# Block 2's convolution as products on TensorE, with another order of the mixers' other work and all weight splits on VectorE

## The chip, the cores and the metric

The kernel runs on one core of a Trainium2 chip. The metric is the device time of one execution in microseconds (us). Engines are named as in the profile: PE is TensorE (matrix products), PEld its loading of weights, DVE is VectorE, ACT is ScalarE, POOL is GpSimd, SP is the engine whose queue issues the loads. PEclk is the granted clock of TensorE as a share of its full 2.4 GHz; 0.5 is its lower level, 1.2 GHz.

## The reference

The program is two transformer-like blocks over 256 tokens of width 1024, each followed by a mixture of experts (MoE). The change touches mainly Block 2. There one input projection of the normalised tokens feeds three mixers: a memory cross-attention, a conformer convolution over 384 channels, and a bidirectional RWKV-7 scan. Their outputs are joined, projected, added to the stream, and go into the second MoE. The convolution, cut:

```
def conformer_conv(pc, conv_w, conv_b, ln_g, ln_b):
    val, gate = jnp.split(pc, 2, axis=-1)
    u = val * jax.nn.sigmoid(gate)
    u = lax.conv_general_dilated(u, conv_w[:, None, :], window_strides=(1,),
        padding=[(CONV_PAD, CONV_PAD)], ..., feature_group_count=CONV_WIDTH) + conv_b
    ...
    return jax.nn.silu(uf)
```

It is depthwise: each of the 384 channels has its own 31 taps over the tokens, 15 to either side, and channels don't mix.

## The kernel before

**Stages.** Block 1's projections and mixers run to about 470 us of the trace, its MoE from 450 to 925, Block 2's mixers from 925 to 1265, the second MoE from 1265 to the end. Both MoE stages stream expert weights from HBM in pieces of 1 MB.

**Projections.** `dense_T` and `dense_N` compute in fp32 accuracy by splitting both operands into a high and a low part: three products for each tile (high by high, low by high, high by low). The weights' halves come from `split_w`: ScalarE copies the loaded weights `wc` into `whi` (L161), and a subtraction (L162) gives `wlo`. A counter, `nsplit`, sends every third subtraction to GpSimd and the others to VectorE.

**Block 2's mixers.** `b2_mixers` writes the instructions. Three pairs of projections (`self.pairs`) come first. Then six RWKV chains (`rw_stages`) of some 43 steps each start at steps 0, 4, 9, 15, 19 and 24. A chain begins with its decay gates (products `ps_lw` at L1794 and L1795, tanh at L1798), builds matrices from them, solves small triangular systems by repeated products (`ps_lv`, `rAW`, `rX`), and ends in outputs of 64 columns (`ps_Y`, `ps_S`, `ps_YS`). The products of a chain are small, 64x64 in four positions of the array, and VectorE or ScalarE must move each result before the next product can start. From step 1 on, at every second step, one closure of the list `fill` is written between: further pairs of projections, `b2_attention`, `b2_conv_in` and the three `b2_conv_gate` (the convolution's input, 128 channels each, into `U`), later the loads for the output projection, two early pieces of the second MoE, and the router's preparation. From step 17 on each chain step also takes one tap of the convolution.

**The convolution.** `b2_conv_taps(j0, j1)` does one tap for the three groups of 128 channels. Groups 0 and 1 are one multiply and add each on VectorE (L1649). Group 2 is a scaled copy on ScalarE (L1652) and an addition on GpSimd (L1653). The taps' factors are a per-partition scalar in `cwT`, made in `b2_vectors`. `b2_conv_norm` then normalises the channels.

**What sets the order.** The written order is the start; a scheduler over a simulated timeline moves instructions of each engine within what their inputs and buffers allow. SP's queue runs in order: a load that waits for its buffer holds all loads behind it. The second MoE takes its pieces in the ring order `ORDER2`: two from the small pool `early` (slots `a` and `b`), then slots `r` and numbered slots that come free as the mixers end. The last product of the output projection of Block 2 is `psl` at L2150 and L2151.

Of the kernel before, what the change touches and what calls it, by code (L numbers as in the profile page):

```python
# [18 lines left out]
class K:  # L19
    def __init__(self, ctx, tc, ins, out, dbg=None):  # L20
        self.ctx, self.tc, self.nc, self.I, self.out = ctx, tc, tc.nc, ins, out
        self.dbg = dbg or {}
        self.pools = {}
        self.nsplit = 0
        self.order, self.mixing, self.inorder = None, False, False
        self.cst = self.open("cst", 1)
        self.x = self.cst.tile([P, 2, D], FT, name="x")
# [119 lines left out]
    def split_w(self, wt, kc, n):  # L147
# [3 lines left out]
        for k0 in range(0, kc, step):  # L151
# [1253 lines left out]
    def b2_vectors(self):  # L1405
# [27 lines left out]
        self.cwT = c.tile([P, 3, 31], FT, name="cwT")  # L1433
        nc.vector.tensor_copy(self.cwT, pc)
# [28 lines left out]
    def block2(self):  # L1463
# [15 lines left out]
        self.pairs = [(p, self.b2_proj_load(p)) for p in ((9, 10), (0, 3), (6, 7))]  # L1479
# [17 lines left out]
    TAP0, TAP1, TAPN = 17, 17, 1  # L1497

    def b2_mixers(self):

        self.keys = {}
        for pair, wt in self.pairs:
            self.b2_rwkv_proj(pair, wt)
        chains = [(self.OFF[i], self.rw_stages(i % 2, i // 2)) for i in range(6)]
        fill = [lambda: self.b2_rwkv_proj((1, 4)), lambda: self.b2_rwkv_proj((2, 5)),
                lambda: self.b2_rwkv_proj((8, 11)), self.b2_attention, self.b2_conv_in]
        fill += [lambda c=c: self.b2_conv_gate(c) for c in range(3)]
        taps = [lambda j=j: self.b2_conv_taps(j, min(j + 1, 31)) for j in range(31)] + [self.b2_conv_norm]
# [131 lines left out]
    def b2_conv_taps(self, j0, j1):  # L1640
        nc, tp = self.nc, self.tp
        Y = self.cvY
        for j in range(j0, j1):
            for c in range(3):
                u, w = self.U[:, c, j:j + 256], self.cwT[:, c, j:j + 1]
                if j == 0:
                    nc.vector.tensor_scalar(Y[:, c], u, w, self.v2["cvb"][:, c:c + 1], op0=OP.mult, op1=OP.add)
                elif c < 2:
                    nc.vector.scalar_tensor_tensor(Y[:, c], u, w, Y[:, c], op0=OP.mult, op1=OP.add)  # L1649
                else:  # L1650
                    t = tp.tile([P, T], FT, name="cvt", tag="cvt")
                    nc.scalar.activation(t, u, AF.Copy, scale=w)  # L1652
                    nc.gpsimd.tensor_tensor(Y[:, c], Y[:, c], t, op=OP.add)  # L1653
# [727 lines left out]
```

## Time and profile before

| | us |
|---|---|
| median of 3 runs | 1729.07 |
| lowest and highest | 1726.86, 1734.26 |
| the profiled execution | 1733.84 |
| its span in the trace | 1732.1 |

The 1.7 us between the last two lie outside the span. The profiled execution is 4.8 us above the median. Below, a stretch is a piece of the span given by its start and end, busy time is the time in which an engine executed, and a plain fp32 product appears as two records in the trace, a product of split halves as one.

### The profile page before, as it was taken

To read this page: it belongs to the slowest core of one execution; us is meant where nothing else is said; L and a number is where in the kernel's file an instruction comes from. 1 tells how busy PE (TensorE), PEld (TensorE's weight loads), DVE (VectorE), ACT (ScalarE), POOL (GpSimd) and SP (SyncE) were. 2 spreads that over 40 slices of the span, in tenths; PEclk is the share of its full clock that TensorE was granted. 3 is DMA by queue.
4 is the path that set the end of the run, shared out by engine and by line. 5 is a ranking of instruction groups with operands and counts; after the bars stand their busy time and mean duration, and the time that the engine had idled before them with its cause. 6 is when DMAs were issued, how large, how long until landed. Compare 5 with 4: busy or idle time off the path is not lost. (4 is left out here: it accounts for less than half of the span.)

```text
span 1732.1 us, 33693 instructions
## 1 busy us (share of the span) xinstructions
PE 1456.1 (84%) x14455; PEld 993.2 (57%) x14455; DVE 704.6 (41%) x1745; ACT 356.6 (21%) x768; POOL 282.1 (16%) x323
## 2 busy tenths in 40 slices
PE   6989999989699888888888888678979877877775
PEld 3988988779665545544444877567853423323222
DVE  5895646676722111121123776968631101000002
ACT  1432433454001100000001543333210000000001
POOL 2443122233121000000000221441100000000001
PEclk9999999889699999999998988757989987889878
DMA  9555487665889999999996703302689999999996
GB/s 323 175 168 133 137 259 250 219 209 181 352 352 416 416 415 415 416 416 417 416 415 253 193 1 97 125 1 75 248 318 416 417 418 416 419 415 418 417 417 259
DMA packets 188062, 511.91 MB, mean 296 GB/s; under 512 B 13951, under 2 KB 118519, under 8 KB 155142
## 3 DMA queue, kind: packets, MB, share of 16 engines
q1 hardware_dynamic: 178560, 498.11, 75.1%
q10 hardware_dynamic: 8598, 10.98, 2.5%
q8 instruction: 115, 1.88, 0.4%
q0 software_dynamic: 752, 0.63, 0.1%
q14 instruction: 37, 0.30, 0.0%
HBM read 507.07 MB, written 2.62 MB: 294 GB/s over the span
## 5 line engine op out<-in xcount | busy, mean ns | idle before, releaser
L2263 PE MATMUL ps_h<-wp,xg 128*32 128x256 f32 x2048 | 140.6, 412 | 45.1 <-DMA wp<-in_w_e_up_dram 45.0
L161 ACT CAST whi<-wc 128x1024 fp32r<-128x1024 f32 (+2 forms) x111 | 114.2, 1039 | 152.7 <-PE psd L179 95.0
L1229 PE MATMUL ps_h<-wp,xg 128*32 128x128 f32 x4096 | 138.8, 275 | 0.7 <-DVE xg L1222 0.3
L1229 PEld LDWEIGHTS ps_h<-wp,xg 128*32 128x32 f32 x4096 | 109.1, 110 | 49.0 <-issue 39.3
L2263 PEld LDWEIGHTS ps_h<-wp,xg 128*32 128x32 f32 x2048 | 63.3, 115 | 125.4 <-DMA wp<-in_w_e_up_dram 58.2
L162 POOL TENSOR_TENSOR wlo<-wc,whi 128x1024 fp32r<-128x1024 f32 (+1 forms) x37 | 96.7, 2613 | 234.1 <-ACT whi L161 216.7
L2291 PE MATMUL ps_y<-wp,Vm 128*32 128x512 f32 x480 | 108.2, 659 | 29.9 <-DMA wp<-in_w_e_down_dram 13.9
L179 PE MATMUL psd<-hT_hi,wlo 128*128 128x256 f32 x432 | 124.7, 289 | 9.2 <-DVE wlo L162 7.3
L162 DVE TENSOR_TENSOR wlo<-wc,whi 128x1024 fp32r<-128x1024 f32 (+1 forms) x74 | 103.1, 1401 | 61.8 <-ACT whi L161 57.9
L179 PE MATMUL psd<-hT_hi,whi 128*128 128x256 f32 x432 | 126.1, 292 | 0.3
L1263 PE MATMUL acc<-ey,ecw 128*128 128x512 f32 x248 | 121.7, 620 | 4.0 <-PEq L1296 4.0
L179 PE MATMUL psd<-hT_lo,whi 128*128 128x256 f32 x432 | 123.1, 285 | 0.0
L1240 POOL TENSOR_SCALAR ewg<-onehot,W 128x128 f32<-128x128 f32 x64 | 38.3, 609 | 410.4 <-PE ps_t L1242 375.6
L1253 PE MATMUL ps_y<-wp,egT 128*32 128x512 f32 x512 | 76.8, 608 | 23.7 <-DVE ey L1258 22.5
L1258 DVE TENSOR_TENSOR ey<-ps_y,mod 128x512 f32<-128x512 f32 x64 | 44.2, 691 | 121.5 <-PE ps_y L1253 121.5
L179 PEld LDWEIGHTS psd<-hT_hi,wlo 128*128 128x128 f32 x432 | 83.6, 194 | 12.2 <-DVE wlo L162 8.7
L179 PEld LDWEIGHTS psd<-hT_hi,whi 128*128 128x128 f32 x432 | 84.0, 194 | 3.6 <-issue 2.9
L179 PEld LDWEIGHTS psd<-hT_lo,whi 128*128 128x128 f32 x432 | 83.8, 194 | 0.5 <-issue 0.4
L1263 PEld LDWEIGHTS acc<-ey,ecw 128*128 128x128 f32 x248 | 43.2, 190 | 69.4 <-issue 69.4
L2274 POOL TENSOR_SCALAR ewg<-onehot,aff 128x128 f32<-128x128 f32 x32 | 19.1, 609 | 377.4 <-PE ps_t L2276 359.6
L2291 PEld LDWEIGHTS ps_y<-wp,Vm 128*32 128x32 f32 x480 | 18.2, 114 | 91.9 <-DMA wp<-in_w_e_down_dram 36.4
L2295 ACT COPY ey<-ps_y 128x512 f32<-128x512 f32 x15 | 8.8, 586 | 286.0 <-PE ps_y L2291 286.0
(659 smaller groups left out, 2811.8 us busy)
## 6 DMA issues: line engine op xcount, KB each, us to landing
wp<-in_exp_w_dram SPq DMA_DIRECT2D x192, 1024.0 KB, 18.1
wp<-in_w_e_down_dram SPq DMA_DIRECT2D x64, 1024.0 KB, 20.1
wp<-in_w_e_gate_dram SPq DMA_DIRECT2D x62, 1024.0 KB, 20.0
wp<-in_w_e_up_dram SPq DMA_DIRECT2D x62, 1024.0 KB, 19.9
wc<-in_w_in_dram SPq DMA_DIRECT2D x35, 1024.0 KB, 5.7
wc<-in_ada_w_dram SPq DMA_DIRECT2D x16, 1024.0 KB, 9.0
wc<-in_w_in_dram SPq DMA_DIRECT2D x18, 512.0 KB, 7.1
ada<-in_ada_w_dram SPq DMA_DIRECT2D x6, 1024.0 KB, 13.3
```

What stands on the lines that cost most here:

```text
L161: nc.scalar.copy(hi[:, :kk, cs], src)
L162: eng.tensor_tensor(lo[:, :kk, cs], src, hi[:, :kk, cs].bitcast(FT), op=OP.subtract)
L179: mm = lambda w, x, st, sp: nc.tensor.matmul(ps[:, c], w, x, start=st, stop=sp, skip_group_check=True)
L1229: nc.tensor.matmul(ph[32 * j:32 * j + 32, i], xg[:, 4 * kk + k, 32 * el:32 * el + 32], w[:, k, j * P:(j + 1) * P], start=kk + k == 0, stop ...
L1240: nc.gpsimd.tensor_scalar(wg[:, t], G[:, t, el].unsqueeze(1).to_broadcast([P, 4, 32]), self.W[:, t, e:e + 1], None, op0=OP.mult)
L1253: nc.tensor.matmul(py[32 * j:32 * j + 32], gT[:, 32 * j:32 * j + 32], w2[j // 2][:, j % 2, hf * 512:hf * 512 + 512] if e < 31 else w2[hf][ ...
L1258: nc.vector.tensor_tensor(y[:, hf], py, self.g2[:, hf * 512:hf * 512 + 512], op=OP.mult)
L1263: nc.tensor.matmul(acc[t][hf], cw[:, t], y[:, hf], start=e == 0, stop=False, skip_group_check=True)
L2263: nc.tensor.matmul(ph[32 * j:32 * j + 32], xg[:, 2 * kk + k, 32 * el:32 * el + 32], w[:, k, j * 256:(j + 1) * 256], start=kk + k == 0, sto ...
L2274: nc.gpsimd.tensor_scalar(wg[:, t], G[:, t, el].unsqueeze(1).to_broadcast([P, 4, 32]), self.W[:, t, e:e + 1], None, op0=OP.mult)
L2291: nc.tensor.matmul(py[32 * j:32 * j + 32], gT[:, c, 32 * j:32 * j + 32], w2[j][:, c, hf * 512:hf * 512 + 512], start=c == 0, stop=c == 1, ...
L2295: nc.scalar.copy(y[:, hf], py)
```

## The change

Five things change.

- In `split_w` every subtraction goes to VectorE; the counter is gone.
- `b2_vectors` puts the taps into `cT`, padded to 32, and sixteen small products gather them into `cwS`: partition 32i+r of `cwS` holds, for channel r of a group of 32, the taps of which the index leaves i when divided by four.
- The taps are gone. `b2_conv_shifts` makes copies of `U` in SBUF by DMA: four shifts (by 0 to 3 tokens) of each group of 32 channels stand on the 128 partitions of `cvR`, in the buffers of slots `a` and `b`. That is 16 transfers of 32x3x284 fp32, 109 KB each, from SP's queue.
- `b2_conv_chunk(c)` does 128 channels: two GpSimd products of 128x512 spread the taps to diagonal blocks `W`, then 32 products (128 rows by 32 columns by 256 tokens, plain fp32, in four column positions) accumulate in `ps_cv`, and one ScalarE operation adds the bias. With three chunks that is 96 products, 192 records.
- The list `fill` has another order, and the first pairs too. The projections and gates come first, then the shifts, then the attention, then the three chunks.

```
     def split_w(self, wt, kc, n):
...
-            self.nsplit += 1
-            eng = nc.vector if self.nsplit % 3 else nc.gpsimd
...
-                eng.tensor_tensor(lo[:, :kk, cs], src, hi[:, :kk, cs].bitcast(FT), op=OP.subtract)
+                nc.vector.tensor_tensor(lo[:, :kk, cs], src, hi[:, :kk, cs].bitcast(FT), op=OP.subtract)
...
-        self.pairs = [(p, self.b2_proj_load(p)) for p in ((9, 10), (0, 3), (6, 7))]
+        self.pairs = [(p, self.b2_proj_load(p)) for p in ((0, 3), (9, 10), (6, 7))]
...
-        fill = [lambda: self.b2_rwkv_proj((1, 4)), lambda: self.b2_rwkv_proj((2, 5)),
-                lambda: self.b2_rwkv_proj((8, 11)), self.b2_attention, self.b2_conv_in]
-        fill += [lambda c=c: self.b2_conv_gate(c) for c in range(3)]
-        taps = [lambda j=j: self.b2_conv_taps(j, min(j + 1, 31)) for j in range(31)] + [self.b2_conv_norm]
-        fill += [self.b2_out_loads, self.b2_early_pieces, self.b2_router]
+        g, k = [[lambda c=c, f=f: f(c) for c in range(3)] for f in (self.b2_conv_gate, self.b2_conv_chunk)]
+        fill = [lambda: self.b2_rwkv_proj((1, 4)), lambda: self.b2_rwkv_proj((8, 11)), self.b2_conv_in, g[0], g[1],
+                lambda: self.b2_rwkv_proj((2, 5)), g[2], self.b2_conv_shifts, self.b2_attention, *k]
+        fill += [self.b2_conv_norm, self.b2_out_loads, self.b2_early_pieces, self.b2_router]
...
-                    if step >= self.TAP0 and step % 2 == 0 or step >= self.TAP1:
-                        for _ in range(self.TAPN):
-                            if taps:
-                                taps.pop(0)()
...
-    def b2_conv_taps(self, j0, j1):
...
+    def b2_conv_shifts(self):
+
+        R = [self.early.tile([P, 2, 3, 284], FT, name=f"cvR{i}", tag=f"w{'ab'[i]}", bufs=1) for i in range(2)]
+        for q in range(4):
+            for i in range(4):
+                self.load(R[q // 2][32 * i:32 * i + 32, q % 2], self.U[32 * q:32 * q + 32, :, i:i + 284])
+        self.cvR = lambda c, q, m: R[q // 2][:, q % 2, c, 4 * m:4 * m + T]
+
+    def b2_conv_chunk(self, c):
+
         nc, tp = self.nc, self.tp
...
+        W = []
+        for h, tag in enumerate(("me", "meT")):
+            w = tp.tile([P, 4, 4, 32], FT, name=f"cvW{h}", tag=tag, bufs=1)
+            nc.gpsimd.tensor_tensor(w, self.cwS[:, :, c, 4 * h:4 * h + 4].unsqueeze(3).to_broadcast([P, 4, 4, 32]),
+                                    self.id32.unsqueeze(1).unsqueeze(1).to_broadcast([P, 4, 4, 32]), op=OP.mult)
+            W.append(w)
+        ps = self.pc.tile([P, T], FT, name="ps_cv", tag="c")
+        for m in range(8):
+            for q in range(4):
+                nc.tensor.matmul(ps[32 * q:32 * q + 32], W[m // 4][:, q, m % 4], self.cvR(c, q, m), start=m == 0,
+                                 stop=m == 7, skip_group_check=True, tile_position=(0, 32 * q))
+        nc.scalar.activation(self.cvY[:, c], ps, AF.Identity, bias=self.v2["cvb"][:, c:c + 1])
```

The lines of the changed kernel stand four lower from `split_w` on, and eight higher behind the convolution. Three places in the order of the instructions:

VectorE in one group of Block 1's projections, before; `wlo` are weight splits, the others the group's gates and keys.

```order
L534 SCALAR_TENSOR_TENSOR pr<-f,zc 128x512
L536 COPY PL<-pr 128x16
L538 RECIPROCAL rp<-pr 128x512
L514 TENSOR_TENSOR hgV<-psn,hgV 128x2x256
L162 TENSOR_TENSOR wlo<-wc,whi 128x1024 x2
L542 TENSOR_TENSOR ke<-hgK,PL 128x512
L509 TENSOR_SCALAR hgQ<-psd,vT 128x256 x2
L162 TENSOR_TENSOR wlo<-wc,whi 128x1024 x2
L525 TENSOR_SCALAR f<-th,fB,fA 128x256
```

The same place in the changed kernel.

```order
L158 TENSOR_TENSOR wlo<-wc,whi 128x1024
L530 SCALAR_TENSOR_TENSOR pr<-f,zc 128x512
L510 TENSOR_TENSOR hgV<-psn,hgV 128x2x256
L532 COPY PL<-pr 128x16
L534 RECIPROCAL rp<-pr 128x512
L158 TENSOR_TENSOR wlo<-wc,whi 128x1024 x2
L505 TENSOR_SCALAR hgQ<-psd,vT 128x256 x2
L538 TENSOR_TENSOR ke<-hgK,PL 128x512
L158 TENSOR_TENSOR wlo<-wc,whi 128x1024 x3
L521 TENSOR_SCALAR f<-th,fB,fA 128x256
```

A group now has more splits in VectorE's row, one of them ahead of the scan `pr` (L534 before, L530 now).

SP's queue in Block 2, before; the twelve narrower `wc` are the weights of the three convolution gates, `wc` 128x8x256 the attention's, `Vm` the router's weights in the buffer of the attention's values, `wo` and `wol` the output projection's, `wp` the first pieces of the second MoE.

```order
L61 DMA wc<-in_w_in_dram 128x8x128 x6
L61 DMA wc<-in_w_in_dram 128x8x256
L61 DMA Vm<-in_w_router_dram 128x8x16
L61 DMA wc<-in_w_in_dram 128x8x128 x6
L61 DMA wo<-in_w_out_dram 128x7x256 x4
L61 DMA wol<-in_w_out_dram 128x1024
L61 DMA wp<-in_w_e_gate_dram 128x2048 x2
```

The same place in the changed kernel.

```order
L60 DMA wc<-in_w_in_dram 128x8x128 x12
L60 DMA wc<-in_w_in_dram 128x8x256
L60 DMA cvR_10694<-cvUY 32x3x284 x8
L60 DMA cvR_10695<-cvUY 32x3x284 x8
L60 DMA Vm<-in_w_router_dram 128x8x16
L60 DMA wo<-in_w_out_dram 128x7x256 x4
L60 DMA wol<-in_w_out_dram 128x1024
L60 DMA wp<-in_w_e_gate_dram 128x2048 x2
```

The router's load `Vm`, which must wait for the attention's last product, stood ahead of half of the gates' weights; now it stands behind all of them and behind the sixteen copies.

TensorE from the decay gates of chain 2 (`ps_lw`) on, before; `ps_ms`, `ps_mpt` and `ps_mo` are the attention's products, the others those of the chains.

```order
L1794 MATMUL ps_lw<-pf_9388,ups 128x256
L1795 MATMUL ps_lw<-pf_9388,ups 128x256
L1596 MATMUL ps_ms<-KmT,mq 128x256 x2
L1835 MATMUL ps_lv<-rAW,rX 64x64 x16
L1612 MATMUL ps_mpt<-idn,me 128x128
L1596 MATMUL ps_ms<-KmT,mq 128x256 x2
L1612 MATMUL ps_mpt<-idn,me 128x128 x3
L1835 MATMUL ps_AT<-rar,rbk 64x128 x16
L1835 MATMUL ps_lv<-rAW,rX 64x64 x8
L1876 MATMUL ps_an<-idn,rar 128x128 x2
L1881 MATMUL ps_bk<-idn,rbk 128x128 x4
L1616 MATMUL ps_mo<-meT,Vm 64x256 x2
```

TensorE from the decay gates of chain 2 on, in the changed kernel; `psd` are projections.

```order
L1802 MATMUL ps_lw<-pf_9408,ups 128x256
L1803 MATMUL ps_lw<-pf_9408,ups 128x256
L175 MATMUL psd<-h_hi,whi 128x256
L175 MATMUL psd<-h_lo,whi 128x256
L175 MATMUL psd<-h_hi,wlo 128x256
L175 MATMUL psd<-h_hi,whi 128x256
L175 MATMUL psd<-h_lo,whi 128x256
L175 MATMUL psd<-h_hi,wlo 128x256
```

And the place at which the changed kernel's attention ends, in the stretch of chains 3 and 4.

```order
L1611 MATMUL ps_mpt<-idn,me 128x128 x3
L1843 MATMUL ps_YS<-rar,rbk 64x32 x5
L1615 MATMUL ps_mo<-meT,Vm 64x256 x2
L1843 MATMUL ps_S<-rbk,rAT 64x64 x2
L1884 MATMUL ps_an<-idn,rar 128x128 x2
L1843 MATMUL ps_S<-rbk,rAT 64x64 x2
L1659 MATMUL ps_cv<-cvR_10694,cvW_11098 32x256 x2
L1659 MATMUL ps_cv<-cvR_10695,cvW_11098 32x256 x2
L1659 MATMUL ps_cv<-cvR_10694,cvW_11098 32x256 x2
L1659 MATMUL ps_cv<-cvR_10695,cvW_11098 32x256 x2
L1659 MATMUL ps_cv<-cvR_10694,cvW_11098 32x256 x2
L1659 MATMUL ps_cv<-cvR_10695,cvW_11098 32x256 x2
```

The attention has left the stretch after chain 2's gates, projections stand there, and the attention and the first convolution products stand between chain 4's.

## Rows read from the trace of the kernel before

**Rows 1.** The page, the profiled execution's span

```profile
span 1732.1 us, 33693 instructions
```

**Rows 2.** The busy time by stretch: stretch, length, each engine, PEclk, DMA share, GB/s

```profile
50.00:130.00 80.00, 72.77 (x608) 70.73 (x607) 69.84 (x84) 31.72 (x38) 33.55 (x17) 1.00 0.52 160
130.00:330.00 200.00, 191.66 (x1850) 170.85 (x1851) 116.94 (x262) 73.74 (x163) 45.20 (x25) 0.97 0.67 199
500.00:900.00 400.00, 347.10 (x4549) 204.96 (x4547) 77.41 (x191) 31.20 (x85) 34.29 (x58) 1.00 1.02 416
1003.00:1066.00 63.00, 51.51 (x468) 40.99 (x467) 41.92 (x112) 24.15 (x61) 10.55 (x16) 0.78 0.21 52
1066.00:1151.00 85.00, 61.32 (x711) 52.44 (x710) 75.61 (x177) 35.11 (x75) 36.60 (x42) 0.73 0.21 75
1151.00:1257.00 106.00, 97.11 (x1208) 85.45 (x1206) 74.62 (x244) 28.15 (x58) 14.47 (x15) 0.80 0.37 137
1300.00:1700.00 400.00, 320.11 (x2530) 120.39 (x2528) 33.50 (x71) 19.99 (x45) 17.18 (x29) 0.87 1.02 417
```

**Rows 3.** The chain that ended last: start, length in us, engine and line

```profile
1257.19 0.47 PE psl L2150 x2
...
1305.63 3.63 PE ps_h L2263 x64
...
1686.18 20.08 DMA wp<-in_w_e_up_dram
```

**Rows 4.** The timeline of ACT, decay gates of chains 1, 3 and 5

```profile
1003.40 0.48 ACT L1798 ACTIVATE rwa<-ps_lw,half_w 128x256 f32<-128x256 f32 x1
...
1066.30 0.47 ACT L1798 ACTIVATE rwa<-ps_lw,half_w 128x256 f32<-128x256 f32 x1 [0.68 <-PE ps_lw L1795]
...
1150.51 0.48 ACT L1798 ACTIVATE rwa<-ps_lw,half_w 128x256 f32<-128x256 f32 x1 [1.42 <-PE ps_lw L1795]
```

**Rows 5.** The costliest groups between 40 and 470 us

```profile
L179 PE MATMUL psd<-hT_hi,wlo 128*128 128x256 f32 x432 | 124.7, 289 | 9.2 <-DVE wlo L162 7.3 <-POOL wlo L162 1.9
...
L162 DVE TENSOR_TENSOR wlo<-wc,whi 128x1024 fp32r<-128x1024 f32 x59 | 85.6, 1459 | 45.4 <-ACT whi L161 41.6 <-PE psd L419 3.8
...
L162 POOL TENSOR_TENSOR wlo<-wc,whi 128x1024 fp32r<-128x1024 f32 x29 | 76.9, 2653 | 190.4 <-ACT whi L161 179.0 <-PE psn L198 9.5 <-issue 1.9
```

**Rows 6.** The timeline of VectorE, a weight split with nothing beside it

```profile
78.23 1.22 DVE L162 TENSOR_TENSOR wlo<-wc,whi 128x1024 fp32r<-128x1024 f32 x1 [1.91 <-ACT whi L161]
```

**Rows 7.** The groups between 50 and 130 us

```profile
L536 DVE COPY PL<-pr 128x16 f32<-128x16 f32 x4 | 7.5, 1875 | 0.1
...
L539 POOL TENSOR_TENSOR hgQ<-hgQ,pr 128x512 f32<-128x512 f32 x4 | 5.1, 1286 | 1.7 <-DVE pr L534 1.7
...
L531 DVE COPY zc<-f 128x16 f32<-128x16 f32 x4 | 0.7, 174 | 0.0
```

**Rows 8.** The groups between 925 and 1265 us

```profile
L1649 DVE SCALAR_TENSOR_TENSOR cvUY<-cvUY,cwT 128x256 f32<-128x256 f32 x60 | 35.3, 605 | 0.2
...
L1653 POOL TENSOR_TENSOR cvUY<-cvUY,cvt 128x256 f32<-128x256 f32 x30 | 24.5, 818 | 22.1 <-ACT rE L1824 13.0 <-ACT cvt L1652 7.7
...
L1719 DVE SCALAR_TENSOR_TENSOR pf<-raw,vT,pf 128x256 f32<-128x256 f32 x12 | 6.0, 517 | 0.0
```

**Rows 9.** The busy time by stretch: three shorter stretches of the mixers

```profile
1010.00:1060.00 50.00, 39.02 (x372) 29.55 (x371) 33.71 (x96) 18.89 (x50) 6.49 (x10) 0.76 0.26 65
1104.00:1169.00 65.00, 47.33 (x466) 40.27 (x467) 49.16 (x131) 24.41 (x56) 31.48 (x40) 0.50 0.12 48
1170.00:1240.00 70.00, 62.63 (x886) 54.49 (x886) 52.21 (x164) 20.14 (x43) 8.91 (x9) 0.83 0.34 122
```

**Rows 10.** The timeline of SP's queue: start, time issuing, transfers

```profile
1102.94 0.92 SPq L61 DMA_DIRECT2D wp<-in_w_e_gate_dram  x2
1190.35 29.32 SPq L61 DMA_DIRECT2D wp<-in_w_e_up_dram  x2
```

**Rows 11.** The DMA issues between 1030 and 1110 us: KB, median us to landing

```profile
wc<-in_w_in_dram SPq DMA_DIRECT2D x6, 512.0 KB, 6.3
```

More of the change, by code (lines that the diff above doesn't have):

```diff
@@ L23, in __init__ @@
         self.pools = {}
-        self.nsplit = 0
         self.order, self.mixing, self.inorder = None, False, False
@@ L1432, in b2_vectors @@
             nc.tensor.transpose(pc[:, i], cw[:, i * P:(i + 1) * P], self.idn[:31, :31])
-        self.cwT = c.tile([P, 3, 31], FT, name="cwT")
-        nc.vector.tensor_copy(self.cwT, pc)
+        cT = self.mt.tile([P, 3, 32], FT, name="cwT", tag="eth")
+        nc.vector.memset(cT, 0.0)
+        nc.vector.tensor_copy(cT[:, :, 0:31], pc)
+        pq = self.pm.tile([P, 4, 3, 8], FT, name="ps_cq", tag="t")
+        for q in range(4):
+            for i in range(4):
+                nc.tensor.matmul(pq[32 * i:32 * i + 32, q], self.idn[:, 32 * q:32 * q + 32], cT[:, :, i::4],
+                                 start=q == 0, stop=True, skip_group_check=True, tile_position=(0, 32 * i))
+        self.cwS = c.tile([P, 4, 3, 8], FT, name="cwS")
+        nc.vector.tensor_copy(self.cwS, pq)
     def mean_square(self, sp, x, tag, jk=None):
@@ L1496 @@
     FIRST, EVERY = 1, 2
-    TAP0, TAP1, TAPN = 17, 17, 1
     def b2_mixers(self):
@@ L1522, in b2_mixers @@
             if step == n - 8:
-                for f in fill + taps:
+                for f in fill:
                     f()
@@ L1621, in b2_conv_in @@
         self.uy = uy = self.big([P, 2048], name="cvUY")
-        self.U = uy[:, 0:858].rearrange("p (c t) -> p c t", c=3)
+        self.U = uy[:, 0:861].rearrange("p (c t) -> p c t", c=3)
         self.cvY = uy[:, 1024:1792].rearrange("p (c t) -> p c t", c=3)
         self.nc.gpsimd.memset(self.U[:, :, 0:15], 0.0)
-        self.nc.gpsimd.memset(self.U[:, :, 271:286], 0.0)
+        self.nc.gpsimd.memset(self.U[:, :, 271:287], 0.0)
     def b2_conv_gate(self, c):
@@ L1638, in b2_conv_gate @@
         nc.vector.tensor_tensor(self.U[:, c, 15:271], ps[:, 0], th, op=OP.mult)
-    def b2_conv_taps(self, j0, j1):
-        nc, tp = self.nc, self.tp
[L1642 to L1653, printed above, removed]
+    def b2_conv_shifts(self):
+        R = [self.early.tile([P, 2, 3, 284], FT, name=f"cvR{i}", tag=f"w{'ab'[i]}", bufs=1) for i in range(2)]
+        for q in range(4):
+            for i in range(4):
+                self.load(R[q // 2][32 * i:32 * i + 32, q % 2], self.U[32 * q:32 * q + 32, :, i:i + 284])
+        self.cvR = lambda c, q, m: R[q // 2][:, q % 2, c, 4 * m:4 * m + T]
+    def b2_conv_chunk(self, c):
+        nc, tp = self.nc, self.tp
+        W = []
[6 more added lines that the diff above has]
+        for m in range(8):
+            for q in range(4):
+                nc.tensor.matmul(ps[32 * q:32 * q + 32], W[m // 4][:, q, m % 4], self.cvR(c, q, m), start=m == 0,
+                                 stop=m == 7, skip_group_check=True, tile_position=(0, 32 * q))
+        nc.scalar.activation(self.cvY[:, c], ps, AF.Identity, bias=self.v2["cvb"][:, c:c + 1])
     def b2_conv_norm(self):
```

## The prediction

> **What bounds the kernel now.** I read four views in this order: the span, the busy time by stretch, the chain that ended last, and the groups by line. The span is 1732.1 us [rows 1]. In the two MoE stretches, 500 to 900 and 1300 to 1700, the DMA share is 1.02 at 416 and 417 GB/s [rows 2]: there the weights' stream sets the time, and the chain of the end lies on its transfers [rows 3]. A second stream of fixed length that starts when the mixers free its buffers means that what the mixers' end gains, the end gains one for one. So three pieces of the program count: Block 1's projections (TensorE busy 73 of 80 us between 50 and 130, VectorE 70, so both are near full), Block 2's mixers, and nothing of the two streams.
>
> I cut the mixers at the decay gates, where a new chain begins: chain 1 at 1003.40, chain 3 at 1066.30, chain 5 at 1150.51 [rows 4], and at the last products of the output projection, 1257.19 [rows 3]. That gives A = 1003 to 1066 (63 us), B = 1066 to 1151 (85 us), C = 1151 to 1257 (106 us). What ends last differs among them [rows 2]. In C TensorE is busy 97 of 106 us. In B VectorE is busy 75.6 of 85 us and TensorE 61.3, and in A neither is full (51.5 and 41.9 of 63): there the chains wait for their own round trips between engines. TensorE's records per us say it in one number: A 468/63 = 7.4, B 711/85 = 8.4, C 1208/106 = 11.4. The stretch of the attention, 1010 to 1060, has 372/50 = 7.4 [rows 9].
>
> **The change part by part.** Counts of records of the changed kernel are from its order of instructions, split at the same products; the durations are of the trace.
>
> *Weight splits.* A split on VectorE with nothing beside it takes 1.22 us [rows 6], one on GpSimd 2.65, and the 59 of Block 1 on VectorE take 1.46 in the mean [rows 5], 59 x 0.24 = 14 us more than alone. The copy `PL` of 128x16 takes 1.88 us, another copy of that size 0.17 [rows 7]: four of those lose 6.8 us. I read both as VectorE held up by GpSimd's splits, the only long work on GpSimd there. The change moves 29 splits, 29 x 1.22 = 35 us, to VectorE and takes back at least 14 + 7 = 21, so VectorE gains 14 us of work over 430 us. That costs nothing by itself where TensorE leads, and `wlo` made TensorE wait 9.2 us in all [rows 5]; half of that should go, for a moved split ends 1.4 us sooner. I take +4 us (gain is positive). Bounds: +9 if the whole wait goes; below, 130 to 330 and beyond have 21 moved splits, 26 us on a VectorE that is busy 117 of 200 us [rows 2], and a fifth of that uncovered gives -5.
>
> *The taps' removal, on VectorE, ScalarE and GpSimd.* 60 operations, 35.3 us of VectorE, and 24.5 us of GpSimd [rows 8] go, nearly all of VectorE's inside B. VectorE's 75.6 us in B become some 40. The attention's work comes into B in their place. While it ran in A, VectorE was busy 33.7 of 50 us with the chains' work included [rows 9], and at that share B would have 57 of 85: no bound any more.
>
> *A.* It loses the attention and gets projections: 526 records, of which 215 are `psd`. A projection record costs 72.77/608 = 0.12 us [rows 2], so 215 x 0.12 = 25.8. The other 311 are the chains'. Their pace lies between 7.4 per us (A now) and 12.7 (the best stretch, 1170 to 1240: 886/70 [rows 9]); I take 10, nearer C's 11.4, because the attention's long steps no longer stand between them: 31.1. The first gates come behind 246 `psd` in place of 220, 26 x 0.12 = 3.1 us later. A becomes 25.8 + 31.1 + 3.1 = 60.0, **+3**; at 7.4 it is 71 (-8), at 12.7 it is 53.4 (+10).
>
> *B.* 709 records, no projection, 78 of the convolution. The convolution's products have the shape of `ps_h` in the second MoE (128 rows, 32 columns, 256 tokens, four column positions): 64 records in 3.63 us [rows 3], 0.057 each, 78 x 0.057 = 4.4 us. The other 631 at 10 per us are 63.1. B becomes 67.5, **+17.5**. At 7.4 (attention's pace, since the attention is in B now) it is 89.7 (-5), at 12.7 it is 54.1 (+31). This term decides the forecast; I take 10 since B loses VectorE's taps, the resource that is fullest there, and has no products that fill the array for long.
>
> *C.* It gets 114 records of the convolution, 114 x 0.057 = 6.5, and 19 others, 19/11.4 = 1.7, and loses about one and a half GpSimd splits' wait, 1.5 x 2.65 = 4 [rows 5]: 6.5 + 1.7 - 4 = 4.2 longer, **-4**. At half clock (twice 6.5) and with no wait gone it is -15; if the products go into the 9 us in which TensorE is idle there, 0 to +4.
>
> *What I cost at nothing.* The sixteen tap-gathering products and `cwS` run in Block 1's MoE, whose stream has the DMA share of 1.02 [rows 2]. The sixteen copies wait for the third gate, then issue: 0.46 us each by the first gate pieces [rows 10], 7.4 us, and land some 6.3 us later [rows 11], 14 in all; the order puts the attention, 50 us in the trace [rows 9], between them and the first convolution product. If that cover is gone, the first chunk waits up to 14 us, and the chains pass it. The pieces `wp` behind them on SP's queue now wait for the last convolution product, since the copies hold slots `a` and `b`; before, the first two went at 1102.94, but the next only at 1190.35 [rows 10], and the DMA share in C is 0.37 [rows 2], so two late pieces have room.
>
> *The diagonal blocks.* Six GpSimd products of 128x512; the nearest row is `hgQ`, 1.29 us each [rows 7], 7.7 us. GpSimd is free for them. The Trainium skill, "SBUF — State Buffer", section "Who interferes with whom", says that GpSimd and VectorE share a pair of ports under an exclusive lock; by that rule VectorE would stand still for all 7.7 us, and the sum below would be 7.7 lower, 12.8. The rows show less of it here: beside 24.5 us of taps on GpSimd, VectorE's taps took 605 ns against 517 for the same operation at L1719 [rows 8], 60 x 0.088 = 5.3 us lost, a fifth of GpSimd's time. So I take 1.6 us on a VectorE that has room, nothing on the path.
>
> **The sum.** A 3 + B 17.5 + C -4 + Block 1 4 = 20.5 us. The profiled execution took 1733.84 (span 1732.1 and 1.7 outside), so it becomes 1713.3; the median of the runs is 4.8 below it, and I forecast against that: 1729.07 - 20.5 = **1708**.
>
> **The rivals.** *Fast chains.* With VectorE free the chains run at the pace of the best stretch in A and B, 12.7 per us: 10 + 31 - 4 + 4 = 41, 1688. For it: 1170 to 1240 has the same kinds of product. Against it: there two to three chains and the output projection's wide products overlap, which B doesn't have.
>
> *The attention fills the room.* The attention's round trips (scores, maximum, exponential, transposes, values) are only moved from A to B, and hold B's pace between 7.4 and 8.4 per us. At 8.4 B is 631/8.4 + 4.4 = 79.5 (+5.5), in all +8.5, 1720; at 7.4 it is -5, in all -2, 1731. Middle 1726. For it: the chains, not VectorE's total, may set B's pace. That the taps then bring nothing would be seen in a VectorE that is idle a third of B while the gates keep their distance.
>
> *The clock falls.* Between 1104 and 1169 the granted clock was 0.50, the lower level, with TensorE busy 47 of 65 us on chains alone; before it, with projections in A, it was 0.76 to 0.78, and again 0.83 when the output projection's wide products run [rows 2, 9]. The change takes the last projections out of B. If all of B runs at the lower level, at that stretch's 466/65 = 7.2 records per us: 631/7.2 = 87.6, the convolution at twice its price 8.9, together 96.5 (-11.5), C at twice the convolution's price -11. With A +3 and Block 1 +4: -15.5, 1745, slower. It decides if B's granted clock is under about 0.6. The Trainium skill, "TensorE: Matmul & The Clock Gate", section "Why this matters for your kernels", advises against idle gaps between bursts of products because they put the clock back to half its rate; the row of 1104 to 1169 agrees with it. Against this rival: a faster chain has smaller gaps, and the convolution brings dense products into B.
>
> *VectorE full in Block 1.* At 70 of 80 us busy with 8 more splits in 50 to 130, 10 us, it becomes the bound if none of its stalls goes. With half of the 35 us moved on the path, Block 1 is -17.5 in place of +4, the sum 20.5 - 21.5 = -1, 1730.
>
> **How the numbers follow.** The forecast, 1693 to 1720: 0.50. Fast chains, 1678 to 1693: 0.18. The attention fills the room, 1720 to 1734: 0.18. The clock falls, 1735 to 1752: 0.10. VectorE full in Block 1: 0.04. A measurement of this kernel can tell about 0.5% from no change, 8.6 us: faster is under 1720.4, slower over 1737.7. Faster: 0.50 + 0.18 and 0.02 of the third, 0.70. Same: 0.16 and 0.03 of the last, with 0.01 of the fourth, 0.20. Slower: 0.10. The range goes from 1680 to 1734: it leaves out the clock's case, a little of the fast chains' and some of the rest, together under 0.2.
>
> **What would show it.** In the profile of after: no tap lines, and chain 3's to chain 5's gates 60 to 75 us apart in place of 84, with VectorE under 65 us busy between them; chain 1's to chain 3's gates at 58 to 62. The convolution's records at 0.05 to 0.07 us each with the first one soon behind the attention. `PL` back near 0.17 us and `wlo` at 1.22 in Block 1, with the first MoE's stream starting 0 to 9 us sooner. The last product of the output projection 15 to 25 us earlier and the end with it. It is wrong if B's clock falls under 0.6, if the gates keep their distance although VectorE has room, if TensorE waits for `wlo` more than 9.2 us in Block 1, or if the second stream does not start as much earlier as the mixers end.

## The result, and the profile after

The changed kernel takes 1711.3 us in the median of 8 runs (1710.1 to 1722.5), beside 1730.7 of the kernel before in 8 runs: a ratio of 0.9891, 95% interval 0.9869 to 0.9912, 18.9 us less. The forecast was 20.5 less. The profiled execution took 1710.15 us. Single runs of one kernel spread here over 6 to 22 us, the longer ones at a lower mean granted clock (in the twelve of e11 the three longest have 0.901 to 0.904, the others 0.905 to 0.920), so ratios are given with their intervals.

The page of after, its span [rows 1]:

```profile
span 1708.5 us, 34045 instructions
```

The busy time by stretch of after [rows 2]: stretch, length, then PE, PEld, DVE, ACT and POOL busy with their records, PEclk, DMA share, GB/s. The three in the middle are A, B and C by after's own gates.

```profile
50.00:130.00 80.00, 77.83 (x671) 77.22 (x670) 74.00 (x100) 34.77 (x43) 19.81 (x13) 1.00 0.60 168
130.00:330.00 200.00, 194.55 (x1892) 172.81 (x1891) 127.63 (x290) 80.23 (x179) 12.11 (x10) 0.98 0.70 213
...
500.00:900.00 400.00, 344.67 (x4323) 197.69 (x4323) 74.53 (x185) 30.18 (x82) 31.90 (x54) 0.99 1.01 411
...
996.60:1045.60 49.00, 47.03 (x527) 42.17 (x526) 38.67 (x96) 21.45 (x45) 8.01 (x10) 0.95 0.19 49
1045.60:1119.70 74.10, 66.62 (x714) 48.90 (x717) 42.60 (x129) 21.80 (x57) 10.29 (x14) 0.69 0.19 59
1119.70:1236.00 116.30, 103.97 (x1349) 87.58 (x1350) 76.73 (x249) 31.07 (x66) 10.10 (x14) 0.82 0.43 163
...
1280.00:1680.00 400.00, 317.23 (x2528) 119.45 (x2530) 33.04 (x70) 19.15 (x43) 15.98 (x27) 0.88 1.02 417
```

The timeline of ACT of after, the decay gates of chains 1, 3 and 5 [rows 4]:

```profile
996.56 0.46 ACT L1806 ACTIVATE rwa<-ps_lw,half_w 128x256 f32<-128x256 f32 x1
...
1045.64 0.47 ACT L1806 ACTIVATE rwa<-ps_lw,half_w 128x256 f32<-128x256 f32 x1 [1.56 <-PE ps_lw L1803]
...
1119.72 0.47 ACT L1806 ACTIVATE rwa<-ps_lw,half_w 128x256 f32<-128x256 f32 x1 [3.05 <-PE ps_lw L1803]
```

A shrank from 62.9 to 49.1 us, B from 84.2 to 74.1. C, to the end of the last product of the output projection (1260.0 before, 1236.5 after), grew from 109.5 to 116.8. In B VectorE is busy 42.6 us in place of 75.6, as forecast, and TensorE now 66.6 of 74.1. The second stream is as fast as before (417 GB/s, share 1.02), and the time from the last product to the end is 472.0 against 472.1: the mixers' end moved the end one for one.

All profiled executions, cut at the same events: the first product of the first MoE's experts (`ps_x`), the last of that stage (`acc`), the gates of chains 1, 3 and 5, the last product of the output projection, the end. In us:

| kernel | Block 1 | first MoE | to gates | A | B | C | rest | span |
|---|---|---|---|---|---|---|---|---|
| before | 473.2 | 473.5 | 56.7 | 62.9 | 84.2 | 109.5 | 472.1 | 1732.1 |
| after | 454.1 | 485.1 | 57.4 | 49.1 | 74.1 | 116.8 | 472.0 | 1708.5 |
| e1, splits | 456.2 | 486.2 | 56.4 | 63.5 | 83.5 | 105.9 | 472.5 | 1724.2 |
| e5, convolution | 474.8 | 471.8 | 57.3 | 59.9 | 68.0 | 125.6 | 473.0 | 1730.3 |
| e3, order | 473.0 | 473.3 | 52.7 | 78.4 | 74.4 | 103.4 | 471.9 | 1727.0 |
| e2, convolution and order | 473.7 | 476.1 | 51.0 | 58.7 | 76.1 | 126.4 | 472.9 | 1734.8 |
| e4, splits and convolution | 454.2 | 484.1 | 57.7 | 57.0 | 63.6 | 122.0 | 472.2 | 1710.8 |
| e6, splits and order | 455.8 | 486.6 | 56.1 | 73.4 | 67.2 | 112.3 | 471.9 | 1723.3 |
| e7, GpSimd splits in Block 2 only | 456.2 | 485.1 | 51.8 | 61.5 | 74.0 | 113.7 | 472.6 | 1714.9 |
| e8, GpSimd splits in Block 1 only | 475.5 | 471.8 | 57.9 | 49.1 | 73.9 | 116.8 | 472.2 | 1717.1 |
| e9, first MoE in before's order | 461.9 | 471.9 | 57.4 | 49.1 | 74.1 | 116.7 | 471.9 | 1702.9 |
| e10, first MoE's groups whole | 456.0 | 472.6 | 56.1 | 49.0 | 74.0 | 116.7 | 472.0 | 1696.4 |
| e11, after again | 456.7 | 485.9 | 57.2 | 47.5 | 75.1 | 116.7 | 471.9 | 1710.9 |
| e12, e10 again | 454.7 | 474.9 | 57.3 | 49.1 | 74.0 | 116.7 | 471.9 | 1698.6 |

The table says at once what the median hides: Block 1 became 19.1 us shorter, the first MoE 11.6 longer, and the mixers (A to C) 16.6 shorter. A single profiled run has its scatter: before and after are 23.6 us apart here where the ratio gives 18.9, Block 1 of e9 took 7.8 us longer than after's with the same instructions in the same order, and the rows of e4, e6, e9 and e10 are each the fastest run of its kernel, that of e1 the slowest.

### The profile page after: what moved, and what is told of

Same layout as the page of the kernel before. It is cut to its first block, busy times and chain, and to the rows that moved or that the text cites. A ratio compares the mean times of both kernels' runs of the same rounds, so it can differ in the third digit from the quotient of the medians.

```text
span 1708.5 us, 34045 instructions
## 1 busy us (share of the span) xinstructions
PE 1465.0 (86%) x14679; PEld 987.0 (58%) x14679; DVE 678.7 (40%) x1725; ACT 343.4 (20%) x741; POOL 173.0 (10%) x258
## 5 line engine op out<-in xcount | busy, mean ns | idle before, releaser
L158 DVE TENSOR_TENSOR wlo<-wc,whi 128x1024 fp32r<-128x1024 f32 (+2 forms) x111 | 141.5, 1289 | 50.0 <-ACT whi L157 45.4
L1249 PE MATMUL ps_y<-wp,egT 128*32 128x512 f32 x512 | 84.0, 613 | 23.6 <-DVE ey L1254 22.4
L1229 ACT ACTIVATE eth<-ps_h 128x128 f32<-128x128 f32 x32 | 8.9, 277 | 309.0 <-PE ps_h L1225 309.0
L1210 PE MATMUL ps_x<-onehot,mod 128*128 128x128 f32 x256 | 65.6, 412 | 4.7 <-DVE onehot L1183 3.5
L1210 PEld LDWEIGHTS ps_x<-onehot,mod 128*128 128x128 f32 x256 | 62.5, 335 | 11.4 <-issue 7.4
```

Of the source, the lines that this page charges most:

```text
L158: nc.vector.tensor_tensor(lo[:, :kk, cs], src, hi[:, :kk, cs].bitcast(FT), op=OP.subtract)
L1210: nc.tensor.matmul(px[:, k], self.z[:, t, 4 * kk + k::8], G[:, t], start=t == 0, stop=t == 1)
L1249: nc.tensor.matmul(py[32 * j:32 * j + 32], gT[:, 32 * j:32 * j + 32], w2[j // 2][:, j % 2, hf * 512:hf * 512 + 512] if e < 31 else w2[hf][ ...
```

## The experiments

**Which edit carries it.** The change is three edits: splits on VectorE, the convolution as products, and the order. Six kernels have one or two of them; before and after are the corners.

e1 is the kernel before with the splits alone.

```
-                eng.tensor_tensor(lo[:, :kk, cs], src, hi[:, :kk, cs].bitcast(FT), op=OP.subtract)
+                nc.vector.tensor_tensor(lo[:, :kk, cs], src, hi[:, :kk, cs].bitcast(FT), op=OP.subtract)
```

> The kernel before with one edit: all weight splits on VectorE. Theory (the splits give Block 1's gain and are worth some 7 us at the end): the first MoE's router ends 15 to 19 us sooner than the 465.5 us of before, the first decay gates 5 to 9 us sooner than 1003.4, the end at 1720 to 1726, ratio 0.994 to 0.998. Rival (the stream of the first MoE gives all of it back, so the change's gain is Block 2's alone): router sooner, first gates and end unchanged within 3 us, ratio 0.998 to 1.002.

Measured: 0.9929 (0.9900 to 0.9958), 12.3 us less. The router's products end at 448.6 us, 16.9 sooner, chain 1's gates only 4.6 sooner. The rival falls; the theory's mechanism holds, though the gates gained a little less than expected and the end a little more.

e2 is the changed kernel without that edit.

```
+            eng = nc.vector if self.nsplit % 3 else nc.gpsimd
```

> The changed kernel with every third weight split back on GpSimd. Theory: Block 1 as before (router at 463 to 467 us, first gates within 3 us of 1003), mixers as in the changed kernel (gates of chain 1 to last product of the output projection 238 to 243 us, against 256.6 before), end at 1715 to 1720, ratio 0.990 to 0.995. Rival (splits give nothing at the end): 1709 to 1713, as the changed kernel.

Measured: 1.0007 (0.9979 to 1.0035). Neither fits: convolution and order together, without the splits, are worth nothing. Chain 5's gates are 15.0 us sooner than before, and C takes all of it back (126.4 against 109.5).

e3 is the kernel before with the new order, taps kept; e6 the same with the splits.

```
-                lambda: self.b2_rwkv_proj((8, 11)), self.b2_attention, self.b2_conv_in]
+                lambda: self.b2_rwkv_proj((8, 11)), self.b2_conv_in, g[0], g[1],
+                lambda: self.b2_rwkv_proj((2, 5)), g[2], self.b2_attention]
```

> The kernel before with the changed kernel's order of first pairs and of fill, the taps kept on VectorE, ScalarE and GpSimd. Theory (the order gives A its 14 us, the products give B its 11): chain 1's gates to chain 3's 48 to 53 us, chain 3's to chain 5's 88 to 100 us since the attention and the taps meet there, end within 6 us of before (1724 to 1736). Rival (the order does it all, the taps were hidden): A 49 us and B 74 to 78, end at 1712 to 1718, ratio 0.989 to 0.993.

> The kernel before with all splits on VectorE and the changed kernel's order, the taps kept. Theory (without the products the new order lets the taps run into A, as it did with splits in thirds, where A was 78.4 us): router 446 to 449, first MoE 484 to 487, A 66 to 78, B 72 to 76, C 102 to 108, end at 1718 to 1730. Rival (A's 49 us come from order and splits, with no part of the products): A 49 to 54, end at 1706 to 1714.

Measured: 1.0026 (0.9992 to 1.0059) and 1.0034 (1.0016 to 1.0053). The order alone gives nothing, and it undoes what the splits give. Both expectations missed: e3 ended where its theory had it, but with A at 78.4 and B at 74.4 us; e6 had A where its theory had it, but B and C off and the end later. The costliest groups of e3 between 999 and 1077 us, its A, say why: line, engine, operation, count, busy us and mean ns.

```profile
L1649 DVE SCALAR_TENSOR_TENSOR cvUY<-cvUY,cwT 128x256 f32<-128x256 f32 x60 | 32.2, 567 | 0.1
```

With the convolution's gates ready sooner all sixty taps of VectorE run in A, which becomes 78.4 us (73.4 in e6). With the convolution off VectorE the same order has A at 58.7 us (e2). e6's median is 1737.0, above what its row in the table says.

e5 is the kernel before with the convolution as products alone, e4 the same with the splits; both keep the attention and the projections where they were.

```
+        fill = [lambda: self.b2_rwkv_proj((1, 4)), lambda: self.b2_rwkv_proj((2, 5)),
+                lambda: self.b2_rwkv_proj((8, 11)), self.b2_attention, self.b2_conv_in, *g, self.b2_conv_shifts, *k]
```

> The kernel before with the convolution as products alone: order of first pairs and fill as before, every third split on GpSimd. Theory (the products free B and cost C, whatever the order): router 465 us, first MoE 473 to 477, A 60 to 64 us, B 62 to 68 against 84, C 118 to 128 against 109.5, end at 1720 to 1731. Rival (the products pay only together with the other edits): B over 76, end at 1730 to 1740.

> The changed kernel with the order of first pairs and fill of before: the attention stays in A, the shifts and the three chunks come behind the third gate, splits all on VectorE. Theory (order and products each give a part): A 60 to 66 us as before, B 62 to 70 us since the taps are gone from a VectorE that was full there, end at 1712 to 1722. Rival (the products bring nothing without the new order, since B's length is the chains' own): B 80 to 85, end at 1722 to 1728 with the splits' part alone.

Measured: 1.0001 (0.9982 to 1.0020) for e5, 0.9916 (0.9885 to 0.9946) for e4. By stage both come out as the theory had it: B falls to 68.0 and 63.6 us, C grows to 125.6 and 122.0. By the end time the products alone are worth nothing. e4 against e1, and after against e4, differ by less than their intervals: on top of the splits, products and order together are worth some 3 to 7 us (0.9912 and 0.9891 in two sets of runs, against 0.9929), about the width of the intervals, and these runs can't divide that.

**Where the splits pay.** e7 has GpSimd splits in Block 2 alone, e8 in Block 1 alone.

```
+            eng = nc.gpsimd if hasattr(self, "w2in") and self.nsplit % 3 == 0 else nc.vector
...
+            eng = nc.vector if hasattr(self, "w2in") or self.nsplit % 3 else nc.gpsimd
```

> The changed kernel, but in Block 2 every third weight split is on GpSimd again; Block 1 keeps them all on VectorE. With GpSimd splits in both blocks the changed kernel's whole gain was gone (ratio 1.0007), and its last stretch, chain 6's gates to the last product, was 104 us against 95. Theory C2 (the GpSimd splits of Block 2 hold up the last stretch): Block 1's router 446 to 448 us, first gates 996 to 998, first gates to the last product 250 to 262 us against 240, end at 1722 to 1732. Rival C1 (Block 2's splits don't matter, and what was lost came from Block 1's): mixers 238 to 244, end at 1709 to 1715.

> The changed kernel, but in Block 1 every third weight split is on GpSimd again; Block 2 keeps them all on VectorE. Theory C2: Block 1's router at 465 to 467 us, the first MoE 475 us long as before, first gates at 999 to 1002, mixers 238 to 244 us, end at 1712 to 1718, so that Block 1's part of the splits is worth 2 to 6 us at the end. Rival C1: mixers 250 to 262, end at 1725 to 1736.

Measured: 0.9923 (0.9888 to 0.9959) and 0.9919 (0.9883 to 0.9956). At the end e7 (median 1717.3) lies between C2 and C1, and e8 (1720.3) 2 us behind what C2 said. In the mixers C2 holds for A, not for C: from the last product of the first MoE to chain 3's gates it is 113.3 us in e7 and 107.0 in e8 (119.6 before, 106.5 after), while C in e7 is even 3 us shorter. Each block's splits give some 13 to 14 us beside the other two edits, which alone give nothing (e2). If the two parts added, the changed kernel would be at 0.984; it is at 0.9891 and, in e11, 0.9912, a difference of about the width of the intervals, so that this is not shown. The profiles have one thing that would not add: a passage of C that takes 29.4 us in e2 takes 17.9 in e7 and 17.6 in e8 (the last part of the next section).

**The first MoE.** Its code is untouched, yet it takes 484 to 487 us in every kernel with Block 1's splits on VectorE (after, e1, e4, e6, e7, e11) and 472 to 476 in every other, those with a pinned order (e9, e10, e12) among them. The order of TensorE's instructions differs there: a group of four column-tile products `ps_y` is cut in halves by other products 13 times, before 7 times. The timeline of TensorE of after shows one cut group and a whole one; a record is half of a product.

```profile
596.75 1.05 PE L1249 MATMUL ps_y<-wp,egT 128*32 128x512 f32 x4
598.57 4.05 PE L1210 MATMUL ps_x<-onehot,mod 128*128 128x128 f32 x16 [0.77 <-DVE onehot L1183]
602.54 1.05 PE L1249 MATMUL ps_y<-wp,egT 128*32 128x512 f32 x4
604.39 1.07 PE L1249 MATMUL ps_y<-wp,egT 128*32 128x512 f32 x8 [0.79 <-DVE ey L1254]
```

The two halves, at 596.75 and 602.54, take 1.05 us each; the whole group at 604.39 takes 1.07. A cut therefore costs about 1 us of TensorE. The costliest groups in the first MoE, `ps_y` of before and then of after:

```profile
L1253 PE MATMUL ps_y<-wp,egT 128*32 128x512 f32 x512 | 76.8, 608 | 23.7 <-DVE ey L1258 22.5 <-DVE egT L1247 1.2
```

```profile
L1249 PE MATMUL ps_y<-wp,egT 128*32 128x512 f32 x512 | 84.0, 613 | 23.6 <-DVE ey L1254 22.4 <-DVE egT L1243 1.1
```

7.2 us more for six more cuts. e9 pins TensorE's order in that stage to that of before, e10 to one in which only one group is cut; nothing else is changed.

```
+                    self.tc.add_manual_dep(ins.ins, prev.ins.name, mybir.DependencyInfo(
+                        mybir.DependencyClass.NoSync, mybir.DependencyReason.DATA), reason="order")
```

> The changed kernel with TensorE's order in the first 29 experts of the first MoE pinned to that of the kernel before; Block 2's order is untouched. In the changed kernel 13 groups of four column-tile products ps_y are cut by other products, before 7, and the stage took 485 us from its first product to its last against 473.5. Theory M1 (the order took it): 473 to 479 us, end 6 to 11 us sooner than the changed kernel, 1700 to 1705. Rival M2 (the stream of weights took it, since it starts sooner and then waits for the same buffers): 483 to 487 us, end at 1709 to 1713.

> The changed kernel with TensorE's order in the first 29 experts pinned so that groups of four column-tile products are never cut (1 cut left in place of 13). Theory M1, at some 1 us for a cut: 467 to 475 us from the first product of the first MoE to the last, unless its stream of weights (191 MB at 416 GB/s, 460 us) becomes the bound, end at 1697 to 1704. Rival M2: 483 to 487 us, end at 1709 to 1713.

Measured: 0.9846 (0.9803 to 0.9888) and 0.9835 (0.9793 to 0.9878); the stage took 471.9 and 472.6 us, the ends (medians 1708.4 and 1707.8) came later than M1 had them. In the stage M1 holds: the order took it. The cuts are not all of it: of the 13.2 us between after and e9, 10.7 are TensorE's busy time (419.4 against 408.7 us), 7.2 of these in `ps_y`, and no run divides the rest. `ps_y` of e10 took 6.6 us less again for six cuts fewer:

```profile
L1258 PE MATMUL ps_y<-wp,egT 128*32 128x512 f32 x512 | 70.2, 601 | 27.6 <-DVE ey L1263 23.5 <-DMA wp<-in_exp_w_dram 3.0 <-DVE egT L1252 1.1
```

But the stage did not follow. What SP's queue waited for between 475 and 900 us, first of before, then of after, then of e10 (total, times, longest):

```profile
SPq L61 <- PE ps_h L1229: 141.5, 69, 9.2
SPq L61 <- DMA wp<-in_exp_w_dram: 133.3, 76, 3.4
SPq L61 <- PE ps_y L1253: 53.1, 23, 7.3
```

```profile
SPq L60 <- PE ps_h L1225: 171.7, 83, 6.3
SPq L60 <- PE ps_y L1249: 116.4, 27, 11.9
...
SPq L60 <- DMA wp<-in_exp_w_dram: 26.5, 19, 2.8
```

```profile
SPq L61 <- DMA wp<-in_exp_w_dram: 247.2, 130, 3.6
SPq L61 <- PE ps_h L1234: 57.3, 38, 5.8
```

In after the loads wait for TensorE to free buffers, and for the most part they did so before; in e10 they wait for earlier transfers. The weights' stream has become the bound, and TensorE's last 6 us save nothing.

**The version that beats both.** e11 is the changed kernel, e12 is e10, again, on one chip.

> The changed kernel once more, to stand beside the next run on one chip: 0.986 to 0.992 of the kernel before.

> The changed kernel with the first MoE's groups of four kept whole, once more. Theory (the first MoE's order is worth 6 to 12 us at the end): 0.980 to 0.986 of the kernel before, and its first MoE 471 to 474 us from its first product to its last in place of 485. Rival (the earlier lower time was the scatter of the runs): within 3 us of the changed kernel beside it.

Measured: 0.9912 (0.9884 to 0.9941) and 0.9836 (0.9807 to 0.9866), medians 1713.0 and 1699.9. The first MoE took 485.9 and 474.9 us. e10 is 28 us faster than before and some 13 faster than the change.

## Why the prediction was right, and where its steps were not

The sum was 20.5 us, the ratio gives 18.9 (the forecast's median, 1729.07 - 20.5, is 1708.6, not 1708). It came out by luck, through errors that cancel. Of the forecast 16.5 us were the mixers' and 4 Block 1's. In the profiles the mixers gave 16.6, but as A 13.8, B 10.1 and C -7.3 where 3, 17.5 and -4 were forecast; Block 1 gave 19.1, and the first MoE took 11.6 of it back. By edit, the splits alone give 12.3, and the other two edits alone or together give nothing. By the prediction's own steps:

- *Weight splits, +4.* The mechanism is right, the size wrong by a factor of five in the profiles, and its own cost was missed. Block 1's costliest groups of after [rows 5]:

```profile
L175 PE MATMUL psd<-hT_hi,wlo 128*128 128x256 f32 x432 | 121.9, 283 | 3.8 <-DVE wlo L158 3.8
L158 DVE TENSOR_TENSOR wlo<-wc,whi 128x1024 fp32r<-128x1024 f32 x88 | 114.2, 1313 | 39.5 <-ACT whi L157 36.1 <-PE psd L415 3.3
```

The wait for `wlo` fell from 9.2 us to 3.8, even more than the half that was taken. But that was the only wait priced. TensorE's idle time of all kinds, from 20 us to the router's last product, fell from 39.6 to 28.6 us: 5.4 are the wait for `wlo`, some 4 the waits for other results of VectorE, whose own busy time grew by 5.5 us and not by 14. TensorE's busy time fell by 8 us with the same number of records. That makes 19. The idle part stands in all nine profiles with Block 1's splits on VectorE (29 to 32 us, against 40 to 44 in the other five). The busy part stands in eight of the nine (396 to 399 us, against 404 to 407); e9 has 405.5 with after's order of instructions, and what sets it stays open. The forecast that `PL` would go back to 0.17 us failed [rows 7]; the groups between 50 and 130 us:

```profile
L535 POOL TENSOR_TENSOR hgQ<-hgQ,pr 128x512 f32<-128x512 f32 x4 | 6.1, 1513 | 53.2 <-DVE pr L530 53.2
...
L532 DVE COPY PL<-pr 128x16 f32<-128x16 f32 x4 | 4.0, 1008 | 0.0
```

`PL` halved. Before, three of the four ran beside a split on GpSimd and took 2.2 us, until the split had ended; the fourth met only the product `hgQ` and took 0.92. In after all four meet `hgQ` (0.90 to 1.27 us). A split of 128x1024 on VectorE takes 1.22 us in the mean where nothing runs on GpSimd, as forecast, and 1.56 beside GpSimd's other work.

- *The first MoE at nothing.* This step failed. It read the stage as bound by the stream, from a DMA share of 1.02 [rows 2]. TensorE was nearly as full (347 of 400 us), and the queue's waits of before, shown above, name TensorE more than earlier transfers (141.5 and 53.1 us against 133.3). The change let the scheduler cut TensorE's groups, and 11.6 of the 19.1 us were given back there (e9, e10).

- *A, 60.0 forecast, 49.1 measured.* The count was right (525 records, 212 of them `psd`), the sum was not. It laid the projections' 25.8 us and the chains' 31.1 end to end, and took the chains' pace from stretches in which TensorE waits for them. In after the projections are busy 27.3 us, the other records 22.1, and TensorE is busy 47.0 of 49.0 us: the projections fill the chains' waits. The busy time of `psd` in A of after (TensorE, its loading, VectorE, ScalarE):

```profile
996.60:1045.60 49.00, 27.34 (x214) 25.35 (x212) 1.94 (x4) 2.47 (x6) 0.95 0.19 49
```

The 3.1 us for the later first gates lie ahead of A and did not belong in it; that stretch grew by 0.7. What was also missed is Block 2's own splits, which were costed in C only: with every third on GpSimd (e2, e7) 264 records of `psd` fall into A in place of 212, A is 58.7 and 61.5 us, and from the end of the first MoE to chain 3's gates e7 takes 6.8 us more than after.

- *B, 67.5 forecast, 74.1 measured.* VectorE's relief came as said (42.6 us busy). The pace was 9.4 records per us outside the convolution (636 records in 74.1 - 6.7 us), not 10, and two errors hide in it. The attention's 48 records (`ps_ms`, `ps_mpt`, `ps_mo`) alone kept TensorE busy for 18.9 us, against 15.3 in A of before. The other 588 had 48.5 us, 12 per us, close to the 12.7 of the rival of fast chains. The busy time by stretch of after, through the attention:

```profile
1066.00:1076.00 10.00, 8.14 (x76) 5.95 (x75) 4.91 (x15) 4.50 (x15) 0.29 (x1) 0.59 0.00 0
1076.00:1086.00 10.00, 9.27 (x22) 4.53 (x21) 3.34 (x12) 2.13 (x8) 0.00 (x0) 0.50 0.14 20
1086.00:1096.00 10.00, 8.75 (x62) 5.31 (x63) 6.90 (x16) 4.62 (x10) 2.69 (x3) 0.72 1.09 354
```

The clock was at its lower level or near it in the attention, with 22 records in one 10 us. Where the attention stays in A, B took 63.6 us with 97 records of projections in it (e4): so the attention's move into B is what the pace of 10 left out. The rival of the falling clock came in part, B's clock is 0.69, above the 0.6 at which it would have decided.

- *C, 4 forecast, 7.3 measured.* The timeline of TensorE of after, the first and the last convolution products:

```profile
1095.49 3.24 PE L1659 MATMUL ps_cv<-cvR,cvW 128*32 128x256 f32 x46
...
1142.26 5.60 PE L1659 MATMUL ps_cv<-cvR,cvW 128*32 128x256 f32 x64
```

The first 46 records cost 0.070 us each, the last 64 0.088, most of them at a granted clock of 0.50 (1136 to 1146). The busy time of the convolution's products in B and in C:

```profile
1045.60:1119.60 74.00, 6.65 (x78) 3.26 (x78) 0.69 0.19 59
1119.60:1148.00 28.40, 9.02 (x114) 4.15 (x114) 0.70 0.01 2
```

So C's 114 records took 9.0 us, between the 6.5 taken and the 13 of half clock. But this is not where C grew. Its three parts, cut at the solves of chains 5 and 6 (ScalarE's copy `rR` in `rw_solve`), are 56.4, 17.6 and 42.7 us, against 57.1, 18.4 and 34.1 before. The last part, from chain 6's solve to the last product, before and then in after:

```profile
1225.90:1260.00 34.10, 32.56 (x381) 28.59 (x381) 22.09 (x69) 10.23 (x16) 4.18 (x2) 1.00 0.79 295
```

```profile
1193.70:1236.50 42.80, 41.19 (x429) 37.12 (x429) 24.28 (x76) 10.84 (x19) 0.00 (x0) 0.92 0.71 271
```

TensorE is full in both, and in after it has more left to do: 139 records of the output projection (`psn`) against 111, and 35 of the router (`ps_rl`) against 15. The step that failed is the place of the cost, which was put on the convolution's own products.

- *What was costed at nothing in Block 2* held. SP's queue of after:

```profile
1029.68 11.55 SPq L60 DMA_DIRECT2D cvR<-cvUY  x16
...
1147.90 0.82 SPq L60 DMA_DIRECT2D wp<-in_w_e_gate_dram  x2
1161.45 28.20 SPq L60 DMA_DIRECT2D wp<-in_w_e_up_dram  x2
```

The copies were issued within 11.6 us and the DMA share is back at 0.01 between 1046 and 1066, long before the first convolution product at 1095.49. The early pieces waited for the last convolution product (1147.9), and the next still went 29 us sooner than before [rows 10]. The six diagonal blocks took 1.05 to 1.17 us on GpSimd. Beside them four operations of VectorE took longer than their like with nothing beside them, 2.2 us in all (`rX` 1.13 in place of 0.41, `rE` 1.29 in place of 0.41): near the 1.6 taken, and not 7.7. Whether a chain waited for them is not shown.

So the step that failed most is the division: the mixers' gain was forecast for the convolution and the order, and without the splits C takes it back (e2, e5).

**Where the convolution's gain goes.** e5 is the plainest case: B 16.2 us shorter, C 16.1 longer, end unchanged. Two things make up C's growth. From chain 6's solve to the last product it is 40.2 us against 34.1, with the same 139 records of the output projection left over as in after. And from chain 5's solve to chain 6's it is 29.4 us against 18.4. The busy time of e5 in a stretch of 30 us around that part:

```profile
1185.00:1215.00 30.00, 29.06 (x289) 27.75 (x290) 11.95 (x45) 3.36 (x8) 1.34 (x2) 0.50 0.30 107
```

In that stretch TensorE was busy 29.1 of 30 us at a granted clock of 0.50. e2 has the same, e7 does not. First e2, then e7, the 10 us ahead of the stretch and the stretch itself:

```profile
1182.00:1192.00 10.00, 7.09 (x90) 6.44 (x88) 8.11 (x28) 4.23 (x10) 0.00 (x0) 0.50 0.33 119
1192.00:1221.00 29.00, 28.83 (x287) 27.18 (x284) 12.18 (x51) 3.53 (x8) 1.80 (x3) 0.53 0.25 91
```

```profile
1175.00:1185.00 10.00, 7.09 (x92) 6.44 (x90) 8.31 (x28) 4.22 (x11) 0.00 (x0) 0.50 0.33 119
1185.00:1203.00 18.00, 17.57 (x296) 16.41 (x293) 11.39 (x47) 4.05 (x8) 1.87 (x3) 0.98 0.42 155
```

Both come to it alike: clock 0.50, TensorE busy 7.1 of 10 us while VectorE normalises the convolution. Then e7 gets 0.98 and does 296 records in 18 us, e2 gets 0.53 (0.50 until 1216) and does 287 in 29. In e4 the same step took 23.1 us, in after and in e8 to e12 17.6 to 17.7. For the profiled runs this shows where the time goes that the convolution alone saves in B. What decides the clock there stays open: the kernels differ ahead of it in where the stages stand in time, and no run here varied that alone. Whether the same passage makes the spread of single runs was not seen either: only the changed kernel and e10 have a second profile (e11, e12), and neither shows it.

## What to carry to other kernels

Price an edit in every stage that holds its operation, and look for what the faster stage hands over to: here a stage that looked bound by its stream had TensorE busy 87% of the time and a load queue that waited for TensorE more than for transfers, and a scheduler that was given another start cut its groups of concurrent products. Do not add up two kinds of work end to end on an engine where one can fill the other's waits. Test the edits of a change one by one: the one that was thought a by-product carried the gain. Where an engine's relief makes one stretch shorter, look for the same time in the next before counting it.

## What the runs showed of the hardware

- TensorE was busy 28.8 of 29 us at a mean granted clock of 0.53, at its lower level until 1216 (e2, 1192 to 1221); the same step of the chains ran at 0.98 in e7. The Trainium skill, "TensorE: Matmul & The Clock Gate", section "Why this matters for your kernels", advises against idle gaps between bursts. This stretch had 0.2 us of them in all, and the clock did not rise for 24 us.
- Four column-tile products, each in its own column position, take 1.07 us as a group and 1.05 us for each half when other products stand between (after, 596 to 605).
- The 128x16 copy `PL` on VectorE took 2.2 us beside a split on GpSimd and 0.9 to 1.3 beside a 128x512 product there; another copy of that size, `zc`, with nothing beside it took 0.17 (before and after, 59 to 126).
